# A seven-product attention/pooling step on one core: eight products in the first two chunks' attention stage, the combined weights made later, and stores moved to GpSimd's DMA queue

## The chip, the cores and the metric

The kernel runs on one core of a Trainium2 chip. The metric is the device time of one execution in microseconds (us). The time before is 2448.59 us, the median of 3 runs (2443.82 to 2450.43). A profiled execution of the same kernel took 2446.67 us.

Engines are named as the profile names them: PE is TensorE (matrix products), DVE is VectorE, ACT is ScalarE, POOL is GpSimd, and SP is SyncE, which in this kernel issues DMAs. Each engine runs its own instruction list strictly in order; an instruction that waits for a semaphore holds up everything behind it on its engine. In the lists, SPq and the like mean the instruction queue of that engine, where DMA issues stand.

## What is computed

One layer of a decoder step over 4096 prompt positions (and 8 single sampled positions), model width 1024, all in float32:

```python
u, zp, q, k, v, za, gp, ga = split_projection(rmsnorm(xp, g_norm[l]), w_in[l])
pooled = multiscale_pool(u, 0, seq)                        # trailing means, windows 2/4/8/16
att = attn_prompt(q, k, v, rel_bias, attn_sinks[l])        # 8 heads of 64, 2 kv heads, window 128, sinks
pg = jnp.einsum('btgc,gce->btge', pooled.reshape(b, t, POOL_GROUPS, POOL_GROUP_DIM), w_grp)
br_pool = jnp.einsum('btp,pd->btd', pg * pool_scale * jax.nn.silu(z_pool), w_br_pool)
br_attn = jnp.einsum('bta,ad->btd', att * jax.nn.silu(z_attn), w_br_attn)
merged = jax.nn.sigmoid(g_pool) * br_pool + jax.nn.sigmoid(g_attn) * br_attn
x + jnp.einsum('btd,de->bte', merged, w_out)               # then a final rmsnorm
```

The input projection `split_projection` is the largest matrix product: 1024 inputs, 4352 output columns. Its columns are cut into tiles of 128, named by their place in one array of weight tiles: `W_U`=0, `W_Z`=4, `W_Q`=8, `W_K`=12, `W_V`=13, `W_A`=14, `W_GP`=18, `W_GA`=34; `W_BR` and `W_O` belong to the two later products.

## The kernel before

**Numbers in two halves.** PE multiplies in a reduced format, so each operand is kept as a high part and a low rest, and every product is made of three matrix passes (`mm3`: high by high, high by low, low by high). The two halves of a weight tile are made by `split_into`: ACT copies the raw float32 tile into the high half (`w[:, 0]`), and DVE (or POOL, where it is told) subtracts to get the low half. The tile `w` (128 partitions, 4 KB each, 512 KB in all) comes from `wtile`: five buffers with the tag `w`, and from the second chunk on three more (`w2`), because `more_weights` closes a first memory pool (`p0`, whose tiles `fst` makes) at the end of the first chunk and opens another in its place.

**Seven products.** The sequence is cut into 8 chunks of 512 positions (the second has 520: the 8 sampled positions ride along). Within a chunk, two weight tiles (`ia`, `ib`) and the two halves of the chunk's columns form a 2 by 2 block product, done by class `Pair` with the Strassen-Winograd scheme: 7 block products rather than 8, each 12 matmuls of 256 columns (260 in the second chunk). `part1` makes four of them, `part2` three. Four of the seven weight operands are sums of quarter tiles: s1 to s4. In the first chunk `combined` loads the four quarters and DVE adds them (line 196); `kept` splits each sum and stores it to DRAM (`ss...`, line 169); from the second chunk on, `kept` loads the finished 512 KB tile with one DMA (line 165) and nothing is added. The other three operands are plain quarters, loaded as 256 KB and split each time (`wquarter`). DVE and ACT put the products of a pair together (lines 267 to 285).

**Order of a chunk.** (1) `K`: the key/value pair, two query pairs, the first attention-gate pair; meanwhile `finish` normalizes and stores the chunk before. (2) `S`, the attention stage: eight steps `hb`. Each does one pair out of `FILL` (`a`, `u`, `z`, `u`, `z`, `gp`, `ga`, `gp`): `part1`, then the earlier steps' value product and transposes, the scores of this step, then `part2`. These are the pairs that the change touches. From the second chunk on they make their low halves on POOL (`att`). Then the pair `ga 1`. (3) `B`: the two output branches for 8 tiles, with the last gate pairs between (`gate_pair`). (4) `O`: the output product, and the next chunk's input (`prep_xt`); in the first chunk its weights are split and stored too (`kept("o...")`).

**What sets the order.** The code names the work in one order, and a scheduler lists it for each engine in another: each instruction is put where its operands and buffers are expected to be free, with the code's order as priority. All DMAs stand in SP's list. Matmul results live in five PSUM buffers (`mm`): a pair in the first chunk takes two, in the second chunk (260 columns don't fit two to a buffer) four, and the scores take two per step.

## Time and profile before

| | before |
|---|---|
| median of 3 runs | 2448.59 us |
| the profiled execution | 2446.67 us |
| its span, first to last instruction | 2444.9 us |
| PE busy | 2363.1 us (97%) |
| DVE busy | 1650.8 us (68%) |
| ACT busy | 1146.0 us (47%) |
| POOL busy | 310.0 us (13%) |
| DMA | 583.60 MB, mean 239 GB/s |
| mean granted PE clock | 0.987 |

Busy time counts each engine by itself, so the four overlap. A busy share is a mean over stages with different limits; the prediction therefore reads windows, which give busy times between two moments of the span. The stages are cut where their first instruction of a kind starts: `K` at the first copy of line 614, `S` at the first score reduction (line 407), `B` at the first branch product (line 801), `O` at the first residual sum (line 847), up to the next chunk's line 614. `S` as cut here with what follows it up to `B` holds the eight steps, the pair `ga 1` and part of the next pair. For the first chunk these moments are 56.4, 96.7, 240.8 and 319.5 us, and the second chunk's are 375.6, 418.7, (end of its eight steps) 518.6, 546.5 and 625.6.

In a row of grouped instructions stand the line, the engine, the operation, output and inputs, the shapes, the count, the busy time, the mean duration in ns, and the idle time ahead of them with what ended it. In a row of waits stand who waited for whom, the total, the count and the longest. In a row of DMA issues stand the count, the size and the median time from issue to landing.

### The profile page before, as it was taken

The page shows a single profiled execution, that of the slowest core. Times are in us where ns is not written, and L with a number is a line of the kernel's source. Part 1 is how long each engine was busy: PE and PEld are TensorE (multiplying, and loading weights), DVE is VectorE, ACT ScalarE, POOL GpSimd, SP SyncE. Part 2 cuts the span into 40 slices and gives each one's busy share as a digit, 9 for nine tenths or more (in the row PEclk, how much of TensorE's full clock was granted, in tenths as well). Part 3 has the DMA queues.
Part 4 walks back from the last instruction along what each step waited for, and adds up shares of the span by engine and source line. Part 5 has one row for each costly group of instructions (what it writes and reads, how often), then busy time and mean ns, then how long its engine had stood idle before and what let it go on. Part 6 is the DMA issues. An engine that isn't in the chain of part 4 may idle for free.

```text
span 2444.9 us, 43970 instructions
## 1 busy us (share of the span) xinstructions
PE 2363.1 (97%) x16551; PEld 2198.0 (90%) x16551; DVE 1650.8 (68%) x3208; ACT 1146.0 (47%) x2324; POOL 310.0 (13%) x258
## 2 busy tenths in 40 slices
PE   7989999999999999999999999999999999999997
PEld 6878879999999988999889998899888998899986
DVE  6998776865668656686566855677556775668652
ACT  4667534563245633465234642456423563245531
POOL 0000001310024000330003300042001410013000
PEclk9989999999999999999999999999999999999998
DMA  6756688876686667767677666776667776687653
GB/s 203 255 194 245 226 282 322 227 244 219 223 279 239 237 231 242 272 232 245 212 256 266 236 229 233 246 267 237 228 233 260 248 239 231 233 279 246 215 196 141
DMA packets 231903, 583.60 MB, mean 239 GB/s; under 512 B 36315, under 2 KB 38652, under 8 KB 231692
## 3 DMA queue, kind: packets, MB, share of 16 engines
q1 hardware_dynamic: 231692, 580.80, 69.3%
q8 instruction: 131, 2.15, 0.3%
q14 instruction: 80, 0.66, 0.1%
HBM read 516.30 MB, written 64.40 MB: 238 GB/s over the span
## 4 chain that ended last, share of the span: by engine, by line
PE 68%; DVE 16%; DMA 7%; ACT 4%; issue 3%; SPq 0%; POOL 0%; DVEq 0%; ACTq 0%; POOLq 0%
PE hb L175 12%; PE hb L177 12%; PE hb L176 12%; PE mm L177 9%; PE mm L175 9%; PE mm L176 8%; DMA H<-in_xt 3%; DMA wr<-in_xq 2%; DVE oy L569 2%; DVE w L137 2%; PE tp L433 2%; PE pv L444 2%; DVE H L675 1%; DVE xt L180 1%; ACT LL L414 1%
## 5 line engine op out<-in xcount | busy, mean ns | idle before, releaser
L175 PE MATMUL hb<-xt,w 128*128 128x256 f32 x3316 | 945.3, 285 | 33.5 <-DVE U L268 13.3
L177 PE MATMUL hb<-xt,w 128*128 128x256 f32 x3316 | 941.4, 284 | 7.0 <-DVE w L137 7.0
L176 PE MATMUL hb<-xt,w 128*128 128x256 f32 x3316 | 938.2, 283 | 3.1 <-DVE xt L180 3.0
L175 PEld LDWEIGHTS hb<-xt,w 128*128 128x128 f32 x3316 | 633.2, 191 | 46.6 <-DVE H L272 15.1
L177 PEld LDWEIGHTS hb<-xt,w 128*128 128x128 f32 x3316 | 632.5, 191 | 10.1 <-DVE w L137 9.9
L176 PEld LDWEIGHTS hb<-xt,w 128*128 128x128 f32 x3316 | 632.8, 191 | 6.1 <-DVE xt L180 4.3
L136 ACT CAST w<-wr 128x512 fp32r<-128x512 f32 x570 | 349.5, 617 | 324.3 <-PE hb L177 202.2
L137 DVE TENSOR_TENSOR w<-wr,w 128x512 fp32r<-128x512 f32 x402 | 275.6, 689 | 141.1 <-ACT w L136 135.8
L137 POOL TENSOR_TENSOR w<-wr,w 128x512 fp32r<-128x512 f32 x168 | 251.6, 1501 | 500.5 <-ACT w L136 409.7
L175 PE MATMUL mm<-mh,w 128*128 128x512 f32 (+1 forms) x576 | 213.8, 371 | 2.4 <-ACT w L136 2.3
L177 PE MATMUL mm<-mh,w 128*128 128x512 f32 (+1 forms) x576 | 213.6, 371 | 0.8 <-DVE w L137 0.8
L176 PE MATMUL mm<-ml,w 128*128 128x512 f32 (+1 forms) x576 | 213.0, 370 | 0.3 <-DVE ml L809 0.3
L297 POOL TENSOR_TENSOR rs<-rs,nhalf 128x4 f32<-128x4 f32 (+1 forms) x18 | 17.9, 999 | 1338.9 <-DVE rs L295 1338.8
L801 DVE SCALAR_TENSOR_TENSOR H<-H,mm 128x512 f32<-128x512 f32 (+1 forms) x144 | 90.3, 628 | 111.9 <-PE mm L177 111.6
L414 ACT ACTIVATE LL<-LL,nm 128x257 f32<-128x257 f32 (+1 forms) x256 | 126.5, 496 | 65.9 <-DVE nm L411 65.8
L175 PE MATMUL mm<-xt,w 128*128 128x260 f32 x476 | 135.9, 286 | 2.0 <-DMA w<-ss 1.3
L177 PE MATMUL mm<-xt,w 128*128 128x260 f32 x476 | 134.8, 284 | 1.1 <-POOL w L137 0.6
L176 PE MATMUL mm<-xt,w 128*128 128x260 f32 x476 | 134.6, 283 | 0.0
L281 DVE TENSOR_TENSOR H<-hb,U 128x512 f32<-128x512 f32 x119 | 81.9, 688 | 73.3 <-PE hb L177 71.0
L175 PEld LDWEIGHTS mm<-mh,w 128*128 128x128 f32 x576 | 108.5, 188 | 22.4 <-ACT w L136 2.8
L177 PEld LDWEIGHTS mm<-mh,w 128*128 128x128 f32 x576 | 108.6, 189 | 22.0 <-DVE w L137 1.9
L847 DVE TENSOR_TENSOR oy<-mm,H 128x512 f32<-128x512 f32 (+1 forms) x72 | 45.1, 630 | 122.9 <-PE mm L177 93.1
(193 smaller groups left out, 4113.8 us busy)
## 6 DMA issues: line engine op xcount, KB each, us to landing
w<-ss SPq DMA_DIRECT2D x476, 512.0 KB, 4.4
wr<-in_wall SPq DMA_DIRECT2D x569, 256.0 KB, 3.4
w<-so SPq DMA_DIRECT2D x112, 512.0 KB, 4.0
ss<-w SPq DMA_DIRECT2D x68, 512.0 KB, 3.2
H<-in_xt SPq DMA_DIRECT2D x32, 512.0 KB, 5.6
wr<-in_xq SPq DMA_DIRECT2D x56, 256.0 KB, 3.0
H<-in_xt SPq DMA_DIRECT2D x56, 256.0 KB, 5.7
out_y<-oy SPq DMA_DIRECT2D x28, 512.0 KB, 4.6
```

What stands on the lines that cost most here:

```text
L136: nc.scalar.copy(w[:, 0], raw)
L137: (eng or nc.vector).tensor_tensor(out=w[:, 1], in0=raw, in1=w[:, 0].bitcast(F32), op=ALU.subtract)
L175: mm(ps, lhsT=w[:, 0, k0 + k, :], rhs=rh, start=start and k == 0, stop=False, **kw)
L176: mm(ps, lhsT=w[:, 0, k0 + k, :], rhs=rl, start=False, stop=False, **kw)
L177: mm(ps, lhsT=w[:, 1, k0 + k, :], rhs=rh, start=False, stop=stop and k == nk - 1, **kw)
L281: nc.vector.tensor_tensor(out=self.mid, in0=self.R, in1=u2.unsqueeze(1).to_broadcast([P, 2, n]), op=ALU.add)
L414: nc.scalar.activation(out=L[:, j, k0:2 * P + 1], in_=L[:, j, k0:2 * P + 1], func=AF.Exp, bias=nm[:, j:j + 1], accum_out=den[:, j:j + 1])
L433: nc.tensor.transpose(tp[:, j, :], L[:, j, kb * P:(kb + 1) * P], ident)
L444: mm(pv, lhsT=vs[:, b + kb, g, :], rhs=pt[:, kb, m].rearrange("p j q -> p (j q)"), start=n == 0 and m == 0, stop=n == len(kbs) - 1 and m == 1)
L569: nc.vector.scalar_tensor_tensor(out=y, in0=y, scalar=gf[:, e:e + 1], in1=rsp[:, 0:n], op0=ALU.mult, op1=ALU.mult)
L801: nc.vector.scalar_tensor_tensor(out=t[:, a:b], in0=t[:, a:b], scalar=1.0, in1=ps, op0=ALU.add, op1=ALU.mult)
L847: nc.vector.tensor_tensor(out=y[:, e % 4, a:f], in0=ps[:, 0:f - a], in1=xt[:, e % 2, a:f], op=ALU.add)
```

## The change

`PLAIN = 2`: in the first two chunks the eight pairs of `S` are made by eight plain block products (`eight1`, `eight2`) with the four raw quarters as operands, each quarter's split tile being used for two products one after the other. They use no sums, so nothing is combined, stored or loaded for them there. In the first chunk DVE makes the low halves, in the second POOL does, as for the other pairs of that stage. Each pair's results are put together by two ACT copies and two DVE additions.

The sums for these eight pairs, needed from the third chunk on, are made by `combine`: four raw loads, four additions, four splits, four stores for each. The code names it eight times in the second chunk: before each of its five gate pairs outside the eight steps, and in three places of its `O`. It uses buffers of its own from the first pool: four raw tiles (`wr0`), one sum (`sr`, made in place), one split tile (`sc`). Therefore `more_weights` now comes at the end of the second chunk, and the second chunk has five `w` buffers.

All stores of `kept` (85 in all: the sums, the pooling weight and the 16 output tiles) and the raw loads of `combine` (32) are issued by POOL; SP has none of them. In the first chunk's other pairs the sum buffer goes from two tiles to one, and s1 is made and used ahead of s2.

```diff
-    def kept(key, make):
-        w = wtile()
+    def kept(key, make, own=False):
+        w = fst([P, 2, 4, P], "sc", 1, F32R) if own else wtile()
...
-        nc.sync.dma_start(out=cache[key], in_=w.bitcast(F32))
+        nc.gpsimd.dma_start(out=cache[key], in_=w.bitcast(F32))
...
-    def combined(ia, ib):
-        odd = len(cache) // 4 % 2
+    def combined(ia, ib, own=False):
+        odd = own or len(cache) // 4 % 2
...
-            nc.sync.dma_start(out=raw[idx, half], in_=i["wall"][idx][:, 4 * half:4 * half + 4, :])
+            (nc.gpsimd if own else nc.sync).dma_start(out=raw[idx, half],
+                                                      in_=i["wall"][idx][:, 4 * half:4 * half + 4, :])
...
-        s1, s2 = [fst([P, 4, P], "sr", 2) for q in range(2)]
+        s = fst([P, 4, P], "sr", 1)
...
-        make = {"s2": lambda: add(s2, s1, a11, ALU.subtract), "s1": lambda: s1,
-                "s3": lambda: add(a21, a11, a21, ALU.subtract), "s4": lambda: add(s2, a12, s2, ALU.subtract)}
+        make = {"s1": lambda: add(s, a21, a22, ALU.add), "s2": lambda: add(s, s, a11, ALU.subtract),
+                "s3": lambda: add(a21, a11, a21, ALU.subtract), "s4": lambda: add(s, a12, s, ALU.subtract)}
...
+        def eight1(self):
+            for q, (p0_, p1_), e in (("11", (self.q6, self.q1), 1), ("21", (self.r5, self.r7), 3)):
+                w = self.w(q)
+                self.prod(p0_, q, B_11, True, w)
+                self.prod(p1_, q, T_1, not self.one, w)
+                nc.scalar.copy(self.q[e], p0_)
+
+        def eight2(self):
+            for q, (p0_, p1_), e in (("12", (self.q6, self.q1), 0), ("22", (self.r5, self.r7), 2)):
+                w = self.w(q)
+                self.prod(p0_, q, B_21, False, w)
+                self.prod(p1_, q, B_22, False, w)
+                nc.scalar.copy(self.q[e], p0_)
+                nc.vector.tensor_tensor(out=self.q[e + 1], in0=p1_, in1=self.q[e + 1], op=ALU.add)
+            return self.h
...
+    def combine(ia):
+        make, _ = combined(ia, ia + 1, True)
+        for q in ("s1", "s2", "s3", "s4"):
+            kept(f"{q}_{ia}", make[q], True)
...
+        later = [first_tile(*f) for f in FILL] if c == PLAIN - 1 else []
...
+            if later:
+                combine(later.pop(0))
             x = gate(which, p)
...
+            x = Pair(c, idx, idx + 1, off=16 if what == "u" else 0, eng=att, plain=c < PLAIN)
...
-        if c == 0:
-            more_weights()
...
+            if later and e in (1, 4, 7):
+                combine(later.pop(0))
+        if c == PLAIN - 1:
+            more_weights()
```

**How the lists move.** Line numbers from 31 on are a little higher in the changed kernel: 138 is the low half (before 137), 137 the high half (136), 170 the store (169), 192 the raw load (191), 198 the sums (196), 255, 262 and 263 the putting together in `eight1` and `eight2`.

First, DVE in the first chunk's attention stage, some twelve rows around the end of one pair. Before (the sums are rows with `sr`, the low halves rows of line 137):

```order
L196 TENSOR_TENSOR sr_1218<-wr_1210,wr_1212 128x512
L411 TENSOR_SCALAR nm_1135<-mx_1119 128x4
L196 TENSOR_TENSOR sr_1219<-sr_1218,wr_1214 128x512
L196 TENSOR_TENSOR wr_1210<-wr_1214,wr_1210 128x512
L417 RECIPROCAL rc_1142<-den_1137 128x4
L395 COPY LL_853<-skb 128x4
L281 TENSOR_TENSOR H_1038<-hb_1037,U_134_1039 128x2x256
L137 TENSOR_TENSOR w_1225<-sr_1219,w_1225 128x512
L675 TENSOR_TENSOR H_1199<-H_1038 128x2x527
L137 TENSOR_TENSOR w_1243<-wr_1214,w_1243 128x512
L675 TENSOR_TENSOR H_1200<-H_1199 128x525
L685 TENSOR_TENSOR H_1199<-H_1199,cf 128x16
```

and in the changed kernel:

```order
L448 TENSOR_SCALAR nm_1274<-mx_1258 128x4
L263 TENSOR_TENSOR H_1184<-hb_1182,H_1184 128x256
L138 TENSOR_TENSOR w_1485<-wr_1483,w_1485 128x512
L454 RECIPROCAL rc_1281<-den_1276 128x4
L432 COPY LL_849<-skb 128x4
L263 TENSOR_TENSOR H_1184<-hb_1183,H_1184 128x256
L658 SCALAR_TENSOR_TENSOR H_1349<-H_1349,H_1184 128x2x512
L138 TENSOR_TENSOR w_1516<-wr_1514,w_1516 128x512
L751 SCALAR_TENSOR_TENSOR H_1349<-mm_1359,psc,H_1349 128x512
L751 SCALAR_TENSOR_TENSOR H_1349<-mm_1364,psc,H_1349 128x512
L138 TENSOR_TENSOR w_1564<-wr_1562,w_1564 128x512
L138 TENSOR_TENSOR w_1594<-wr_1592,w_1594 128x512
```

The sums are gone from this stage, and a pair has four low halves where it had seven.

Second, POOL in the second chunk's attention stage. Before, with the low halves of that stage:

```order
L137 TENSOR_TENSOR w_4997<-wr_4995,w_4997 128x512
L137 TENSOR_TENSOR w_5074<-wr_5072,w_5074 128x512
L137 TENSOR_TENSOR w_5174<-wr_5172,w_5174 128x512
L137 TENSOR_TENSOR w_5206<-wr_5204,w_5206 128x512
L673 COPY H_5056<-carry 128x2x16
L627 CAST vs<-vs 128x256
```

and in the changed kernel, with the combining of weight tile 6 (`ss1_6` to `ss4_6` are its four sums in DRAM) among them:

```order
L138 TENSOR_TENSOR w_633_4897<-wr_632_4895,w_633_4897 128x512
L170 DMA ss3_6_6883<-sc_918_6879 128x1024
L732 COPY carry_89<-H_587_4548 128x32
L192 DMA wr0_990_7444<-in_wall 128x512
L138 TENSOR_TENSOR w_647_4971<-wr_646_4969,w_647_4971 128x512
L138 TENSOR_TENSOR w_649_5001<-wr_648_4999,w_649_5001 128x512
L170 DMA ss4_6_6889<-sc_919_6885 128x1024
L192 DMA wr0_1016_7683<-in_wall 128x512
L138 TENSOR_TENSOR w_660_5082<-wr_659_5080,w_660_5082 128x512
```

The code names the combining later, but the scheduler lists it far ahead, since its buffers are free: of the 32 splits into `sc`, 3 stand in the first chunk's `B`, 6 in its `O`, 6 in the second chunk's `K` and 17 among its eight attention steps. POOL's list there holds 32 low halves (before 24) and 17 stores, with the raw loads of the next combining between them.

Third, ACT in the same stage of the changed kernel, over two of the last steps (line 451 is the exponential, 262 and 255 the copies of a pair out of PSUM, 471 the transposed probabilities):

```order
L137 CAST sc_1047_7922<-sr_1046_7921 128x512
L262 COPY H_720_5549<-mm_716_5545 128x260
L137 CAST w_760_5873<-wr_759_5871 128x512
L451 ACTIVATE LL_556_4362,den_733_5650<-LL_556_4362,nm_732_5648 128x257 x4
L262 COPY H_720_5549<-mm_718_5547 128x260
L137 CAST sc_1048_7928<-sr_1046_7921 128x512
L457 ACTIVATE LL_556_4362<-LL_556_4362,rc_734_5655 128x256 x2
L780 ACTIVATE H_720_5549<-H_720_5549 128x2x520
L255 COPY H_743_5728<-mm_739_5724 128x260
L137 CAST w_778_5958<-wr_777_5956 128x512
L255 COPY H_743_5728<-mm_741_5726 128x260
L137 CAST sc_1049_7934<-wr0_1042_7913 128x512
```

Each row with `sc` writes the one `sc` buffer, so it waits until the store of the row with `sc` before it has landed; the PSUM copies and the exponentials stand behind it in ACT's list.

More of the change, by code (lines that the diff above doesn't have):

```diff
@@ L33 @@
 EPS = 1e-6
+PLAIN = 2
 NACT = 2
@@ L204, in split_kernel, with __init__ @@
     class Pair:
-        def __init__(self, c, ia, ib, off=0, eng=None):
-            self.c, self.ia, self.ib, self.eng = c, ia, ib, eng
+        def __init__(self, c, ia, ib, off=0, eng=None, plain=False):
+            self.c, self.ia, self.ib, self.eng, self.eight = c, ia, ib, eng, plain
             self.pre = {}
@@ L212, in __init__ @@
             self.one = 2 * n * 4 <= 2048
-            if c == 0:
+            if c == 0 and not plain:
                 self.make, self.plain = combined(ia, ib)
@@ L224, in __init__ @@
             self.mid = f[:, off + n:off + n + 2 * (SW - n)].rearrange("p (e t) -> p e t", e=2)[:, :, 0:n]
-            self.u2 = st([P, HB], "U2", 2)[:, 0:n]
+            if not plain:
+                self.u2 = st([P, HB], "U2", 2)[:, 0:n]
         def prefetch(self, *names):
@@ L235, in w @@
                 return kept(f"{q}_{self.ia}", self.make[q] if self.c == 0 else None)
-            if self.c == 0:
+            if self.c == 0 and not self.eight:
                 w = wtile()
@@ L274, in part2 @@
         def part2(self):
+            if self.eight:
+                return self.eight2()
             one, u2, n = self.one, self.u2, self.n
@@ L286, in part2, with first_tile @@
             return self.h
+    def first_tile(what, g):
+        if what in ("gp", "ga"):
+            return (W_GP if what == "gp" else W_GA) + 2 * g
+        return {"a": W_A, "u": W_U, "z": W_Z}[what] + g
+    def combine(ia):
+        make, _ = combined(ia, ia + 1, True)
+        for q in ("s1", "s2", "s3", "s4"):
+            kept(f"{q}_{ia}", make[q], True)
     def pair(c, ia, **kw):
@@ L736, in gate @@
         def gate(which, p, **kw):
-            idx = (W_GP if which == "gp" else W_GA) + 2 * p
+            idx = first_tile(which, p)
             return Pair(c, idx, idx + 1, **kw)
+        later = [first_tile(*f) for f in FILL] if c == PLAIN - 1 else []
         def gate_done(which, p, h):
@@ L777, in split_kernel @@
                 next(smp_steps)
+        if later:
+            combine(later.pop(0))
         x = gate("ga", 1)
@@ L871, in split_kernel @@
                 prep_xt(nxt, e // 2)
+            if later and e in (1, 4, 7):
+                combine(later.pop(0))
+        if c == PLAIN - 1:
+            more_weights()
         final = (c, acc, oy, n)
```

23 lines of the change are left out of this document (10 added, 13 removed).

## The prediction

> **What bounds the kernel now.** I read the page's first part, then windows by stage, then PE's waits.
>
> ```profile
> span 2444.9 us, 43970 instructions
> PE 2363.1 (97%) x16551; PEld 2198.0 (90%) x16551; DVE 1650.8 (68%) x3208; ACT 1146.0 (47%) x2324; POOL 310.0 (13%) x258
> ```
>
> PE is busy 97% of the span, so the kernel as a whole is bound by the number of matmuls, and an added matmul is an added time wherever PE doesn't wait. Windows by stage show where it does wait. The columns are the stretch, its length, each engine's busy time with its instructions, the granted PE clock, and the DMA share and rate. In order: the first chunk's `K`, `S` (to `B`), `B`, `O`; the second's `K`, eight steps, and the rest up to `O`; then `S` and `O` of the fourth chunk as a calm measure.
>
> ```profile
> core 0: us, PE busy (x) PEld busy (x) DVE busy (x) ACT busy (x) POOL busy (x), PEclk, DMA share, GB/s
> 56.40:96.70 40.30, 38.64 (x316) 37.28 (x315) 39.49 (x68) 23.49 (x41) 2.33 (x4) 1.00 0.79 283
> 96.70:240.80 144.10, 131.48 (x949) 121.08 (x948) 130.72 (x281) 99.84 (x227) 6.30 (x3) 0.94 0.61 220
> 240.80:319.50 78.70, 78.48 (x463) 68.77 (x462) 63.08 (x108) 39.34 (x73) 2.99 (x6) 1.00 0.61 215
> 319.50:375.60 56.10, 51.18 (x245) 41.37 (x245) 35.59 (x61) 19.05 (x30) 0.63 (x4) 0.97 0.93 335
> 375.60:418.70 43.10, 42.08 (x347) 41.35 (x346) 29.81 (x55) 20.66 (x43) 6.20 (x7) 1.00 0.90 321
> 418.70:518.60 99.90, 97.45 (x785) 94.74 (x784) 74.20 (x189) 57.08 (x138) 31.02 (x27) 1.00 0.77 233
> 518.60:625.60 107.00, 106.61 (x879) 105.81 (x878) 67.11 (x136) 46.82 (x90) 1.01 (x1) 1.00 0.66 225
> 1016.10:1137.80 121.70, 120.89 (x972) 117.72 (x971) 91.45 (x204) 76.42 (x177) 33.60 (x26) 1.00 0.71 244
> 1216.80:1266.80 50.00, 49.89 (x261) 42.26 (x260) 29.95 (x52) 14.63 (x21) 0.00 (x0) 1.00 0.73 247
> ```
>
> The first chunk's `S` takes 144.1 us against 121.7 in the fourth chunk. DVE is busy 130.7 of 144.1 there, PE idles 12.6, and the clock was granted at 0.94, which costs (1 - 0.94) x 144.1 = 8.6 us. Its `O` takes 56.1 against 50.0 with DMA at 0.93. In the second chunk's eight steps PE is busy 97.45 of 99.90: nothing is left to gain there. So the whole loss that this change could take away is some 25 us in the first chunk. What PE waits for in that `S`, and what holds SP's list in the first 376 us:
>
> ```profile
> PE hb L177 <- DVE w L137: 7.0, 6, 3.2
> PE hb L175 <- ACT w L136: 3.7, 7, 1.0
> ...
> SPq L169 <- DVE w L137: 131.7, 72, 11.7
> ```
>
> PE waits for weight halves. The stores in SP's list wait 131.7 us for them in total, with the next loads behind.
>
> **The change part by part.**
>
> *The eighth products* are certain. A product's first and twelfth matmul:
>
> ```profile
> 1040.61 0.28 PE L175 MATMUL hb<-xt,w 128*128 128x256 f32 x1
> ...
> 1041.91 0.28 PE L177 MATMUL hb<-xt,w 128*128 128x256 f32 x1
> ```
>
> Eleven steps take 1.30 us, so a product takes 1.42 us, and one of 260 columns 1.44 (x 260/256, an estimate). Eight pairs cost 11.3 us of PE in the first chunk and 11.5 in the second.
>
> *The first chunk's `S`.* Durations of DVE there, and of ACT's high half:
>
> ```profile
> L137 DVE TENSOR_TENSOR w<-wr,w 128x512 fp32r<-128x512 f32 x29 | 19.8, 687 | 1.1 <-ACT w L136 1.1
> L137 DVE TENSOR_TENSOR w<-sr,w 128x512 fp32r<-128x512 f32 x20 | 13.7, 687 | 3.8 <-ACT w L136 3.7
> L281 DVE TENSOR_TENSOR H<-hb,U 128x512 f32<-128x512 f32 x7 | 4.8, 687 | 2.9 <-PE hb L177 2.9
> L272 DVE TENSOR_TENSOR H<-hb,H 128x256 f32<-128x256 f32 x7 | 2.9, 418 | 0.0
> L268 DVE TENSOR_TENSOR U<-hb,U 128x256 f32<-128x256 f32 x7 | 2.9, 418 | 0.1
> ...
> L196 DVE TENSOR_TENSOR sr<-sr,wr 128x512 f32<-128x512 f32 x7 | 4.8, 689 | 0.1
> ...
> L136 ACT CAST w<-wr 128x512 fp32r<-128x512 f32 x98 | 59.5, 618 | 27.9 <-PE mm L177 11.3 <-DMA wr<-in_wall 8.1 <-PE hb L177 3.7
> ```
>
> A pair loses 4 sums and 3 low halves, 7 x 0.688 = 4.8 us of DVE. Putting it together took 3 x 0.42 + 0.69 = 1.95 us (line 271 as 272) and will take 2 x 0.42, another 1.1 us less. Eight pairs: 47 us. DVE's demand falls from 130.7 to about 84 us and it no longer bounds. At the fourth chunk's pace this stretch is worth 121.7 us, less about 2.7 for the 23 matmuls that the first block lacks (972 against 949, at 0.118 each); with the eighth products 119.0 + 11.3 = 130.3, so 13.8 us less than now. But the pairs `ga 1` and the one after it still combine, so some of the waits stay: I take -12, with -13.8 and -8 as the ends.
>
> *The single sum buffer* puts an ACT copy (0.62 us) between s1 and s2, and the next pair's s1 behind s4. In the first chunk's `K` DVE is busy 39.49 of 40.30 us, so this is on the path: 4 pairs x 2 x 0.62 = 5 us if nothing stands between, less than nothing (PE's 1.7 us idle) if the freed SP list helps more. I take +1. In `B` DVE has 15 us to spare, which hide it and the 3 early splits and their sums (7 x 0.69 = 4.8 us, the price if the cover were gone). Moving the stores gains by itself at most those idle times, since SP's queue is seen by PE only through late halves.
>
> *More transfers where DMA is fullest.* Into the first chunk's `O` go about 4 stores of 0.52 MB and 4 raw loads of 0.26, 3.1 MB; into the second chunk's `K` about 6 and 8, 5.2 MB.
>
> ```profile
> ss<-w SPq DMA_DIRECT2D x37, 512.0 KB, 3.7
> ...
> w<-ss SPq DMA_DIRECT2D x8, 512.0 KB, 7.1
> ...
> GB/s 357 308 316 65 0 171 388 251 346 335 418 388 378 336 146 249 285 163 399 335 224 392 418 426 394 397 340 329 363 399 395 335 257 281 266 319 407 418 426 418
> w<-ss SPq DMA_DIRECT2D x15, 512.0 KB, 5.5
> ```
>
> `O` moves 335 GB/s x 56.1 = 18.8 MB now and will move 21.9; `K` 321 x 43.1 = 13.8, then 19.0. At the best rate of a slice above, 426 GB/s, that is 51 and 45 us, 1.5 more than `K` has. At 335/0.93 = 360 GB/s it is 61 and 53, 14 us more than both have. Below nothing: `O` loses up to its 4.9 us of idle PE if loads no longer stand behind stores. I take +4, nearer to the slices, since stores may land late, but loads then land late too: 5.5 us in that `K`, 7.1 for those issued in `O`.
>
> *Five `w` buffers in the second chunk* give a load the time of 4 products, 5.8 us. A landing of 5.5 fits; one of 7.1 is 1.3 late, for 16 such loads 21 us. After `S` the DMA share was 0.66, so there it is hidden. I take +1, since 5.5 is that stage's own median.
>
> *The second chunk's eight steps*: +11.5. POOL makes 32 low halves there instead of 24 and issues 17 stores and about as many loads among them. Its durations (min/median/max) in the third chunk's steps, and a DVE operation of the same stretch:
>
> ```profile
> L137 POOL TENSOR_TENSOR w<-wr,w x24: 1285/1318/2232, 705.1 to 806.3; 128x512 fp32r<-128x512 f32 x24
> ...
>   ACT w L136: 57.9, 18
> ...
> L423 DVE TENSOR_SCALAR LL<-LL,rc x14: 336/350/1394, 727.2 to 806.4; 128x256 f32<-128x256 f32 x14
> ```
>
> 32 halves are 42 us at the median and 71 if each were the longest. What a DMA issue costs POOL isn't in this trace: from nothing to 1.3 us, a half's price; 35 of them give up to 46 us, and the 111 us of the stage hold 42 and 46. DVE loses 8 x 1.26 us of pair sums (5 x 0.42 against 2) and gets 4.25 combinings, 17 x 2 x 0.69 = 23 us: 74 becomes 88 of 111. Neither is a bound by its sum.
>
> The *chain through the one `sc` buffer* may be. Each link is an ACT copy 0.62, a DVE low half 0.69, a wait behind a POOL half of 0.65 on average, the issue of 0 to 1.3, and the landing, 3.7 in the first chunk's `S`: 5.7 to 7.0 us. The lists place 17 links among the eight steps, 111.4/17 = 6.55 us for each. ACT's copy into `sc` waits for the landing, and the copies that free a pair's PSUM buffers, and the exponentials, stand behind it; PE waits for those. From nothing to 17 x 0.4 = 7 us; I take +4, about the middle.
>
> The rule of the Trainium skill that speaks against this stands in "SBUF — State Buffer", section "SBUF: two separate sides": descriptors of a DMA from GpSimd's queue are written by software through a port pair that VectorE's fast modes lock, and such DMAs should go to SP or ACT. The trace bears out the lock for computing: line 423 takes 0.35 us alone and up to 1.39, in a stretch where POOL's halves take up to 2.23; no run here shows it for descriptors. By it each store could be up to 1 us later, 17 us in the chain.
>
> The sum: +1 - 12 + 0 + 4 + 1 + 11.5 + 4 = +9.5 us, from 2446.67 to 2456.2 us for the profiled execution. The median of the runs stands 1.9 us above that execution, so I predict 2448.6 + 9.5 = 2458 us; 0.3%, about what a measurement of this kernel can tell from no change, is 7.3 us.
>
> **The rivals.**
>
> *All is hidden.* Transfers and chain find room: -13.8 + 11.5 = -2.3 us, 2446 us, not slower. For it: DMA slices of 426 GB/s, ACT busy only 57 of 99.9 us in the second chunk's steps. Against it: 441 GB/s are asked in `K`.
>
> *The chain binds.* A link that also waits once behind another ACT and another DVE instruction of 0.6 takes 8.4 us; (8.4 - 6.55) x 17 = 31 in place of 4 gives +36.5 us, 2485 us. It decides from a link of 6.55 us on. For it: POOL's low halves ahead of a store wait themselves for ACT (57.9 us in 18 waits above). Against it: a pair's PSUM copy has some 2.9 us of slack, two products, before PE needs the buffer.
>
> By the Trainium skill, "DMA: Bandwidth & Descriptors", section "SWDGE vs HWDGE vs iDMA", the descriptors are computed on GpSimd's cores; this would lengthen each link. No run here shows by how much.
>
> *Transfers bind* at 360 GB/s: 14 for the two stages and 5 for late loads, in place of 4 and 1, and nothing for the chain, which waits less where PE is slower: 9.5 + 14 - 4 = +19.5 us, 2468 us. For it: the 0.93 in `O`. Against it: the slices.
>
> *The first chunk gives back everything*: its `S` 13.8, its `O` the 6.1 us above the fourth chunk's, its `K` 1.7, the second chunk pays 11.5: -10 us, 2438.5 us. For it: the 131.7 us of stores ahead of loads in SP's list. Against it: `O` gets more bytes, not fewer.
>
> **How the numbers follow.** The forecast has a chance of 0.35 (its own range 2450 to 2466), "all is hidden" 0.25, "the chain binds" 0.17, "transfers bind" 0.12, "everything back" 0.11. Slower by over 0.3% (above 2455.9): two thirds of the forecast, the chain and the transfers, 0.53. Faster (below 2441.2): 0.11, the last case. Within: 0.36. The range 2440 to 2481 leaves out the upper part of the chain's case and the lower part of the last, about 0.2 together.
>
> **What would show it.** In the first chunk's `S`: near 132 us, DVE busy under 90, no granted clock under 0.97. The second chunk's eight steps: near 115 us; if ACT's waits for stores of `sc` lead PE's waits there, the chain binds. First `O` and second `K`: 56 to 62 and 43 to 46 us; more means transfers. From the third chunk on nothing should move by over 2 us. The forecast is wrong in sign if the first chunk's `S` falls below 125 us, or if its `O` falls to 50.

## The result, and the profile after

The changed kernel takes 2490.53 us (median of 4 runs, 2486.44 to 2491.14), and the kernel before, beside it, 2446.97 us (4 runs, 2443.82 to 2450.43): a ratio of 1.0174, 95% interval 1.0155 to 1.0193. It is slower by 43.6 us, where the prediction said 9.5; 2490.5 lies above the range (2440 to 2481). The page's first lines of the kernel after, whose profiled execution is the source of all rows of "after" below:

```profile
span 2489.4 us, 44409 instructions
PE 2381.9 (96%) x16743; PEld 2221.8 (89%) x16743; DVE 1659.2 (67%) x3176; ACT 1164.0 (47%) x2372; POOL 383.7 (15%) x383
```

PE's busy time rose by 18.8 us (2381.9 against 2363.1), the span by 44.5. So more than half of the loss is PE waiting. The windows by stage, cut as those of before: the first chunk's `K`, `S` (to `B`), `B`, `O`; the second's `K`, eight steps, and the rest up to `O`.

```profile
57.70:99.90 42.20, 38.37 (x306) 36.53 (x305) 37.23 (x61) 24.11 (x43) 7.21 (x15) 1.00 0.68 244
99.90:231.50 131.60, 130.00 (x1047) 126.53 (x1047) 96.21 (x216) 89.24 (x215) 7.93 (x12) 1.00 0.35 123
231.50:322.70 91.20, 81.74 (x462) 70.34 (x462) 68.65 (x117) 42.32 (x80) 18.22 (x34) 0.96 0.67 236
322.70:387.00 64.30, 53.05 (x247) 44.30 (x247) 42.59 (x73) 22.74 (x37) 13.87 (x30) 0.87 0.93 342
387.00:439.90 52.90, 43.19 (x331) 41.43 (x330) 35.05 (x56) 22.94 (x48) 12.98 (x17) 0.97 0.85 309
439.90:566.10 126.20, 115.40 (x889) 111.75 (x888) 98.13 (x204) 74.13 (x176) 57.40 (x63) 0.96 0.54 172
566.10:675.40 109.30, 108.22 (x893) 107.41 (x892) 70.13 (x140) 49.74 (x95) 1.57 (x2) 1.00 0.68 230
```

Against the rows of before: the first `S` is 12.5 us shorter, and then `B` is 12.5 longer, `O` 8.2, the second `K` 9.8, and the eight steps 26.3. From the third chunk on only the `K`s and one `O` (the fifth chunk's, 54.2 before and 50.2 after) move by over 2 us; they differ by up to 4 us either way with the clock granted in them (a late `K` takes 39.7 to 39.8 us at 1.00 and 43.2 to 43.5 at 0.92), in the runs below too. So one stage of one profile is read to some 3 or 4 us, no closer.

### The profile page after: what moved, and what is told of

It is laid out like the page before. It is cut to its first block, busy times and chain, and to the rows that moved or that the text cites. A ratio compares the mean times of both kernels' runs of the same rounds, so it can differ in the third digit from the quotient of the medians.

```text
span 2489.4 us, 44409 instructions
## 1 busy us (share of the span) xinstructions
PE 2381.9 (96%) x16743; PEld 2221.8 (89%) x16743; DVE 1659.2 (67%) x3176; ACT 1164.0 (47%) x2372; POOL 383.7 (15%) x383
## 3 DMA queue, kind: packets, MB, share of 16 engines
q1 hardware_dynamic: 215996, 521.54, 61.6%
## 4 chain that ended last, share of the span: by engine, by line
PE 61%; DVE 9%; DMA 5%; ACT 2%; issue 2%; POOL 0%; SPq 0%; DVEq 0%; ACTq 0%; POOLq 0%
PE hb L176 11%; PE hb L177 11%; PE hb L178 11%; PE mm L176 7%; PE mm L178 7%; PE mm L177 7%; DMA H<-in_xt 2%; DVE oy L606 2%; DMA wr<-in_xq 2%; PE pv L481 2%; PE tp L470 1%; DVE H L712 1%; PE S L439 1%; PE S L440 1%; DVE w L138 1%
## 5 line engine op out<-in xcount | busy, mean ns | idle before, releaser
L138 DVE TENSOR_TENSOR w<-wr,w 128x512 fp32r<-128x512 f32 x402 | 275.5, 687 | 145.3 <-ACT w L137 141.2
L138 POOL TENSOR_TENSOR w<-wr,w 128x512 fp32r<-128x512 f32 x176 | 261.8, 1491 | 468.8 <-ACT w L137 370.1
L334 POOL TENSOR_TENSOR rs<-rs,nhalf 128x4 f32<-128x4 f32 (+1 forms) x18 | 18.7, 1038 | 1228.3 <-DVE rs L332 1228.3
L176 PE MATMUL mm<-xt,w 128*128 128x260 f32 x508 | 149.1, 294 | 19.9 <-DMA w<-ss 14.5
L178 PE MATMUL mm<-xt,w 128*128 128x260 f32 x508 | 147.3, 290 | 1.0 <-POOL w L138 1.0
L177 PE MATMUL mm<-xt,w 128*128 128x260 f32 x508 | 147.0, 289 | 0.0
L177 PEld LDWEIGHTS mm<-ml,w 128*128 128x128 f32 x576 | 108.8, 189 | 21.9 <-DVE ml L847 1.9
```

Of the source, the lines that this page charges most:

```text
L138: (eng or nc.vector).tensor_tensor(out=w[:, 1], in0=raw, in1=w[:, 0].bitcast(F32), op=ALU.subtract)
L176: mm(ps, lhsT=w[:, 0, k0 + k, :], rhs=rh, start=start and k == 0, stop=False, **kw)
L177: mm(ps, lhsT=w[:, 0, k0 + k, :], rhs=rl, start=False, stop=False, **kw)
L178: mm(ps, lhsT=w[:, 1, k0 + k, :], rhs=rh, start=False, stop=stop and k == nk - 1, **kw)
```

## The experiments

Fourteen kernels were run. The table gives the stages of each in us (second chunk: `K`, eight steps, then `Y+B+O`, all that follows up to the third chunk; `Y` is the stretch between the eight steps and `B`). Where the time is a median, the 95% interval of its ratio to the kernel before stands beside it; the others had one run and a profile.

| kernel | time | ratio | K | S | B | O | K 2nd | eight steps | Y+B+O 2nd |
|---|---|---|---|---|---|---|---|---|---|
| before | 2447 | | 40.2 | 144.2 | 78.7 | 56.1 | 43.1 | 99.9 | 161.8 |
| after | 2490.5 | 1.0155–1.0193 | 42.1 | 131.6 | 91.2 | 64.3 | 52.9 | 126.3 | 162.4 |
| 1 stores only on GpSimd | 2466.1 | 1.0068–1.0099 | 41.8 | 149.5 | 82.7 | 59.6 | 45.4 | 102.0 | 162.3 |
| 2 no combining | 2463.8 | 1.0047–1.0101 | 42.1 | 132.3 | 85.6 | 60.1 | 44.3 | 112.9 | 163.9 |
| 3 combining without stores | 2472.2 | | 42.9 | 130.9 | 86.5 | 63.4 | 49.9 | 115.4 | 164.1 |
| 4 combining's DMAs on SP | 2477.3 | | 42.2 | 132.4 | 88.0 | 61.6 | 42.6 | 123.8 | 163.8 |
| 5 all DMAs on SP | 2467.7 | 1.0065–1.0102 | 42.1 | 130.7 | 81.1 | 56.7 | 44.7 | 125.9 | 165.6 |
| 6 no combining, all on SP | 2451.0 | 1.0003–1.0031 | 42.1 | 130.3 | 81.5 | 56.3 | 44.4 | 112.8 | 164.4 |
| 7 stores on ACT's queue | 2484.6 | | 43.9 | 164.0 | 84.0 | 57.8 | 43.4 | 105.2 | 162.7 |
| 8 low halves on POOL | 2453.6 | 1.0005–1.0027 | 41.6 | 148.1 | 80.1 | 56.7 | 43.3 | 99.9 | 161.6 |
| 9 two store buffers | 2482.9 | | 42.1 | 133.2 | 79.7 | 61.6 | 46.1 | 124.0 | 167.6 |
| 10 four pairs, one buffer | 2491.2 | 1.0156–1.0202 | 42.7 | 158.0 | 97.1 | 61.2 | 45.6 | 99.9 | 165.1 |
| 11 three pairs, one buffer | 2480.6 | 1.0105–1.0150 | 42.6 | 167.4 | 88.6 | 56.0 | 44.1 | 100.3 | 162.3 |
| 12 four pairs, shared buffers | 2467.7 | 1.0051–1.0101 | 42.7 | 145.3 | 91.1 | 61.3 | 43.8 | 99.9 | 161.2 |
| 13 combining in shared buffers | 2501.2 | | 42.1 | 130.1 | 80.6 | 56.5 | 45.3 | 112.9 | 212.8 |
| 14 only `O`'s stores on GpSimd | 2456.7 | | 40.2 | 143.7 | 81.8 | 60.4 | 44.4 | 102.1 | 162.1 |

### First round: is it the chain, the queue or the transfers?

Number 1 is the kernel before with one line changed:

```diff
-        nc.sync.dma_start(out=cache[key], in_=w.bitcast(F32))
+        nc.gpsimd.dma_start(out=cache[key], in_=w.bitcast(F32))
```

> The kernel before with one line changed: kept's 85 stores are issued by POOL instead of SP; seven products everywhere, nothing combined later. Theory chain (the loss comes from the combining's 32 splits, one after the other through one sc buffer): no loss here, 2440 to 2450 us, a few us better if SP's loads no longer stand behind stores. Theory queue (a store on POOL's queue is late by itself, and the first chunk waits for it in its w buffers): slower, 2455 us or more, the loss in the first chunk's K, B and O. Theory traffic (bytes where DMA is fullest): the same bytes as before, no change.

It is 19 us slower, by that line alone. The chain theory had said that nothing would come of it, and the prediction too had given this move no loss. Number 2 leaves out the combining (later chunks load another pair's tiles in its place); 3 keeps it without its 32 stores, with the same loads; 4 puts its raw loads and stores on SP:

```diff
-            kept(f"{q}_{ia}", make[q], True)
+            cache[f"{q}_{ia}"] = cache[f"{q}_{W_K}"]        # number 2, and no `combined`
...
+        if own:
+            cache[key] = cache[f"{key[:2]}_{W_K}"]          # number 3, ahead of the store
+            return w
...
+        (nc.sync if own else nc.gpsimd).dma_start(out=cache[key], in_=w.bitcast(F32))   # number 4
```

> The changed kernel without the combining: the 32 combined tiles of the attention stage are never made or stored, and the later chunks load the stored tiles of another pair in their place (same sizes), so the values of those pairs are not the reference's. What is left: eight products in two chunks, stores on POOL, one sum buffer, five w buffers in the second chunk. Chain and traffic: first chunk's attention stage -12.6 us as measured, second chunk's +11.5, little else: 2443 to 2452 us. Theory queue or five w buffers: the loss stays where the ordinary stores or loads are, 2465 us or more, seen in the first chunk's B and the second chunk's K and B.

> The changed kernel with the combining's loads, sums and splits, but its 32 stores left out; the later chunks load another pair's stored tiles, so those pairs' values are not the reference's. Chain: a link loses its landing of some 4.4 us, the lists run through; second chunk's eight steps near 113 us (126 now), first chunk's B near 80 (91), total 2448 to 2460 us. Traffic: two thirds of the added bytes gone, first O and second K give back some two thirds of 18 us, but the second chunk's eight steps, at a DMA share of 0.54, stay above 122: total 2470 to 2480 us. Engine load (sums and splits on DVE and ACT themselves): 2480 us or more.

> The changed kernel with the combining's loads and stores (64 DMAs) issued by SP instead of POOL; the other stores stay on POOL. Chain: a link loses POOL's part (a low half ahead of it, 0.65 us on average, and the issue of 0.56) and some of the landing, but SP's list then holds loads behind stores that wait: 2470 to 2490 us, the eight steps above 118. Queue: the loss is POOL's, so it falls to 2460 us or less.

Number 2 still loses 17 us, where the chain theory wanted 2443 to 2452; at 2463.8 it is just under the queue theory's 2465, and its loss stands in `B` and `O`. Number 3's eight steps fell to 115.4 us, near what the chain theory said, but its time stayed 25 us above before, and its `B` at 86.5 (said: near 80). It doesn't isolate the chain either: without landings to wait for, the scheduler lists the combining earlier. Splits into `sc` that are left in number 3's eight steps, in a list of the tile's instructions (after had 16 there):

```profile
L137 ACT CAST sc<-sr x5: 619/620/623, 430.8 to 455.3; 128x512 fp32r<-128x512 f32 x5
L137 ACT CAST sc<-wr x2: 622/626/629, 433.6 to 448.2; 128x512 fp32r<-128x512 f32 x2
```

Number 4 came out where the chain theory had it (2470 to 2490, eight steps above 118): 2477.3, with the eight steps at 123.8 us. With POOL's queue out of the chain the steps hardly move, so POOL's issue isn't what lengthens them. The second `K`, though, fell from 52.9 to 42.6.

### Second round: the queue taken out of the change

Number 5 is the kernel after with every store and raw load back on SP, number 6 the same without the combining, number 7 the kernel before with its stores on ACT's queue, which like SP's is served by hardware:

```diff
-        nc.gpsimd.dma_start(out=cache[key], in_=w.bitcast(F32))
+        nc.sync.dma_start(out=cache[key], in_=w.bitcast(F32))       # 5 and 6; in 7 nc.scalar
```

> The kernel after, with every store and every raw load back on SP's queue; the eight products, the one buffer for stores of combined pairs and the combining stay. Queue theory (the stores lose 17 to 19 us because on a queue of their own they overlap with the loads that SP goes on to issue, and both land later): the run with the combining's 64 transfers on SP stood at 2477, and the remaining stores' move is worth 17 to 19 of that, so 2456 to 2464, with the first chunk's B back near 80 us and the second chunk's K near 44. Chain theory (what is lost is the one-buffer chain, on whatever queue): 2470 or more, eight steps of the second chunk at 120 us or more and the other stages as in the kernel after. A third way: SP's queue now holds reloads behind stores that wait for the one buffer, and the two effects trade places: 2475 to 2490, with the loss in the second chunk's K and in its eight steps.

> The kernel after without the combining in the second chunk (raw loads, sums, splits and stores of the sixteen attention pairs are left out, and later chunks load another pair's tiles in their place) and with the stores on SP: what is left of the change is eight products for seven in two chunks, the single sum buffer and the order of the head's prefetch. Queue theory: the first chunk's S is 11 to 12 us shorter, the second chunk's eight steps 11 to 13 longer, nothing else moves: 2440 to 2452. Chain theory says the same. Give-back theory (the first chunk's B or O loses what S gains, since its combining and transfers run against the same limit however S ends): 2455 to 2462, with B or O of the first chunk 8 us or more longer.

> The kernel before with its stores issued by ACT and not by SP, nothing else changed. If the loss of the run with the stores alone on GpSimd (19 us) comes from any second queue, because loads no longer wait in line behind stores: 2455 to 2470, B and the second K 3 us or more longer, landing of stores near 4.4 us as there. If it comes from GpSimd (its own issue time, its software queue): within 6 us of before, 2441 to 2453, landing near 3.2 us. ACT also has its own work behind each store that waits for a half; that would show as ACT's waits at the store's line in the eight steps of the later stages.

Windows of number 5, the first chunk's `B`, `O`, the second's `K` and eight steps, and then the eight steps of number 6:

```profile
229.90:311.00 81.10, 79.48 (x464) 68.71 (x464) 68.22 (x117) 42.80 (x79) 4.66 (x5) 1.00 0.75 261
311.00:367.70 56.70, 50.54 (x246) 41.73 (x245) 37.34 (x64) 19.30 (x31) 0.90 (x6) 0.97 0.90 318
367.70:412.40 44.70, 42.07 (x331) 41.07 (x330) 31.07 (x49) 21.61 (x44) 7.91 (x7) 0.96 0.87 295
412.40:538.30 125.90, 115.64 (x893) 111.08 (x892) 95.20 (x201) 73.74 (x175) 43.22 (x35) 0.97 0.59 177
```

```profile
411.50:524.30 112.80, 110.66 (x886) 107.09 (x885) 67.02 (x171) 66.10 (x159) 41.21 (x35) 1.00 0.35 92
```

Number 5 ended between its theories' ranges (to 2464 for the queue, from 2470 for the chain). With everything on SP, `B`, `O` and the second `K` are back within 0.6 to 2.4 us of before; the eight steps keep all of their loss. But its scheduler also listed the combining elsewhere. Splits into `sc` that start in each stage, counted in the traces, and the data moved:

| kernel | `B` | `O` | `K` 2nd | eight steps | later | MB in `B` | MB in `O` | MB in `K` 2nd |
|---|---|---|---|---|---|---|---|---|
| before | 0 | 0 | 0 | 0 | 0 | 17.0 | 18.8 | 13.8 |
| after | 4 | 6 | 5 | 16 | 1 | 21.5 | 22.0 | 16.4 |
| 3 | 6 | 10 | 9 | 7 | 0 | 19.5 | 20.3 | 15.3 |
| 4 | 4 | 4 | 1 | 16 | 7 | 21.4 | 20.0 | 13.2 |
| 5 | 5 | 0 | 1 | 15 | 11 | 21.2 | 18.0 | 13.2 |

So `B` and the eight steps hold nearly the same combining in after and in 5, `O` and the second `K` don't.

Number 6 shows that eight products for seven in two chunks nearly cancel (`S` down 14, eight steps up 12.9, +3.6 in all). After, 5, 2 and 6 are the four cases with and without the combining, with the queue moved or not. From number 6 on: the queue alone adds 12.8 us (2 less 6), the combining alone 16.7 (5 less 6), both together 39.5 (after less 6), 10 more than their sum, which is about the noise of the four medians. The stages show it more sharply: `B`, `O` and the second `K` together take 182.2 us in number 6, 190.0 with the queue alone, 182.5 with the combining alone, and 208.4 with both. Of the 43.6 us, then, some 4 are number 6's, 17 the combining's on SP (13 of them in the eight steps), and 23 come with the queue: 13 of these by itself, the others only with the combining, partly because the scheduler then puts more of it into `O` and the second `K`.

What delays PE in the eight steps is ACT's copies out of PSUM (line 262), which free the buffers that the scores (`S`) need. PE's largest wait there in after and in number 6:

```profile
PE S L439 <- ACT H L262: 6.9, 3, 4.6
```

```profile
PE S L438 <- ACT H L262: 1.6, 1, 1.6
```

Nor is all of the loss waiting. In number 5's eight steps PE is busy 115.6 us for 893 matmuls at a granted clock of 0.97, in number 6's 110.7 for 886 at 1.00; in the first `O` of after 53.1 us for 247 at 0.87, in number 5's 50.5 for 246 at 0.97. Whether PE's waits bring the clock down was not tested.

Number 7 says that late landings aren't GpSimd's software alone. Its time, 2484.6 us, is above the ranges of both theories: `S` grew by 20 us, probably because ACT now waits for halves ahead of each store, so it is no clean price of a second queue. Its `B` also grows by 5.3 us, and its stores land late. Landings in the first chunk's `O` of before, of number 7, and of after, in rows of DMA issues:

```profile
so<-w SPq DMA_DIRECT2D x11, 512.0 KB, 3.0
H<-in_xt SPq DMA_DIRECT2D x6, 256.0 KB, 6.0
```

```profile
so<-w ACTq DMA_DIRECT2D x10, 512.0 KB, 6.4
H<-in_xt SPq DMA_DIRECT2D x6, 256.0 KB, 9.0
```

```profile
so<-w POOLq DMA_DIRECT2D x11, 512.0 KB, 7.5
ss<-sc POOLq DMA_DIRECT2D x6, 512.0 KB, 6.5
wr<-in_wall POOLq DMA_DIRECT2D x7, 256.0 KB, 8.8
```

On a second queue of either kind a store lands after 6.4 to 7.5 us where 3.0 sufficed, and the loads of the next chunk's input on SP land after 9.0 us for 6.0 (the raw weight loads in that `O` didn't change: 5.2 before, 5.1 in number 7). And the loads gained little by it. SP's waits for low halves at its raw loads up to the end of `O`, before and number 1:

```profile
SPq L149 <- DVE w L137: 14.6, 11, 2.8
SPq L191 <- DVE w L137: 10.5, 14, 2.7
```

```profile
SPq L191 <- DVE w L137: 89.6, 34, 9.8
SPq L149 <- DVE w L137: 63.4, 30, 9.5
```

The stores' 131.7 us in SP's list are gone, but the raw loads' waits for the same low halves rose from 25 to 153 us, since a raw tile is free only when its half is made. The stores had mostly held back loads that the buffers hold back anyway.

### A side trial: relief for DVE from POOL

If `S` is bound by DVE, some low halves could simply go to POOL, as in later chunks (number 8):

```diff
-                split_into(w, self.plain[q])
+                split_into(w, self.plain[q], self.eng)
...
-        att = nc.gpsimd if c else None
+        att = nc.gpsimd
```

> The kernel before, with the first chunk's attention pairs left at seven products, but the low halves of the splits of their plain quarters, the sums of their activations and the other operations that the later chunks give to GpSimd given to it in the first chunk too. The first chunk's eight attention steps are bound by VectorE; some 24 low halves of 0.69 us go, 16 us, and TensorE's 110.5 us go toward 99, the length in the second chunk. Queue theory (B lost in the kernel after because of the stores' queue, not because S ended sooner): 2434 to 2441. Give-back theory: the stage behind loses what this one gains: 2444 to 2450. Third: GpSimd becomes late itself, since its split of a half is slower than VectorE's: 2447 to 2455, with the low halves named in the waits of the stage.

`S` grew by 3.9 us. Windows of the first part of `S`, before and number 8, and then grouped instructions of number 8 there:

```profile
96.60:207.10 110.50, 98.87 (x711) 91.37 (x710) 100.50 (x223) 74.22 (x174) 6.30 (x3) 0.92 0.57 207
```

```profile
97.20:208.10 110.90, 94.55 (x707) 88.44 (x708) 99.40 (x203) 73.33 (x174) 34.13 (x24) 0.97 0.58 206
```

```profile
L137 POOL TENSOR_TENSOR w<-wr,w 128x512 fp32r<-128x512 f32 x21 | 33.4, 1602 | 72.4 <-ACT w L136 61.8 <-DVE sza L454 7.4 <-DMA ss<-w 1.9
...
L137 DVE TENSOR_TENSOR w<-sr,w 128x512 fp32r<-128x512 f32 x20 | 17.3, 867 | 6.1 <-ACT w L136 6.0
...
L196 DVE TENSOR_TENSOR sr<-sr,wr 128x512 f32<-128x512 f32 x6 | 5.1, 846 | 0.1
```

Twenty-one halves left DVE, 21 x 0.687 = 14.4 us, but DVE was busy only 1.1 us less (99.4 against 100.5): the mean of its own halves of sums rose from 687 to 867 ns and that of some of its sums from 689 to 846, while POOL's halves took 1602. The trace shows when: ten of the twenty DVE halves `w<-sr` ran beside a half on POOL and took 1049 ns in the mean, the other ten 685. Operations with an input in PSUM (`H<-hb,U`, 687) didn't change. So what POOL took over, DVE gave back in longer operations, and the third theory's range (2447 to 2455) held.

### Third round: the chain against the combining's own work

Number 9 is number 5 with two `sc` buffers, for which one `w` buffer is given up. Numbers 10 and 11 take eight products for only some of the first chunk's pairs, combine those in the first chunk, and leave the second at seven products:

```diff
-        w = fst([P, 2, 4, P], "sc", 1, F32R) if own else wtile()
+        w = fst([P, 2, 4, P], "sc", 2, F32R) if own else wtile()       # 9, with 4 `w` buffers for 5
...
-PLAIN = 2
+PLAIN = 1
+EIGHT = (1, 3, 5, 7)                                                   # 10; in 11 (2, 4, 6)
...
-            x = Pair(c, idx, idx + 1, off=16 if what == "u" else 0, eng=att, plain=c < PLAIN)
+            x = Pair(c, idx, idx + 1, off=16 if what == "u" else 0, eng=att, plain=c < PLAIN and hb in EIGHT)
```

> The run with every store on SP (2467.7, eight steps of the second chunk 125.9), with two buffers for the stores of combined pairs in place of one, and four `w` buffers in place of five, since memory holds no more. Chain theory (each split waits until the store before it has landed): the eight steps fall toward the 115.4 of the run without these stores, 113 to 118, the wait of ACT's high half for the store's landing (16.4 us in eight waits) falls under 5, total 2455 to 2462. Traffic or plain work theory (the 13 us over the run without combining are ACT's, VectorE's and the transfers' own time): 122 or more, 2463 to 2472. If the four `w` buffers bind, the loss shows in other stages of both chunks, above all where the weight loads are waited for.

> Eight products for four of the first chunk's eight attention pairs, every second one; the other four stay at seven. The four are combined in the first chunk itself, through the one buffer, and the second chunk has seven products throughout; every store is on SP, and the second memory pool opens after the first chunk as in the kernel before. The first chunk's S loses 4 x 3.6 us of VectorE (28.6 us went for eight pairs) and gains 4 x 1.4 of TensorE, so 94 to 99 us where before had 110.5. Thirteen of the sixteen splits with their sums, 13 x 1.4 = 18 us of VectorE, stand in Y and B, where VectorE idles 3 + 16 us. Hidden theory: total 2436 to 2443. Give-back theory: Y and B grow by what S loses, 2445 to 2452.

> As the run with four of eight pairs at eight products, with three (the third, fifth and seventh). VectorE loses 10.8 us of 100.5 in the first chunk's S, so 96 to 101 us; twelve splits with their sums, 16.5 us of VectorE, stand behind its scores, ten of them in Y. Hidden theory: 2436 to 2443. Give-back theory: Y is bound by VectorE (30.3 of 33.7 us) and grows by 8 or more, 2443 to 2450.

ACT's wait for landings in the eight steps, after, number 5 and number 9:

```profile
ACT sc L137 <- DMA ss<-sc: 16.5, 8, 4.2
```

```profile
ACT sc L137 <- DMA ss<-sc: 16.4, 8, 4.4
```

```profile
ACT sc L137 <- DMA ss<-sc: 5.6, 3, 4.0
```

The second buffer removed 10.8 us of waits, and the steps became 1.9 us shorter. They hold 19 splits there in place of 15, and PE's wait for ACT's copies (line 262) went from 3.3 us in number 5 to 8.3. The `w` buffer given up shows later: the third chunk's attention steps took 99.8 us for 91.7 and the fourth's 97.7 for 92.9, so the time, 2482.9, lies above both ranges. The run favours the work theory in the eight steps without measuring its share.

Numbers 10 and 11 failed both their theories by more than 25 us, and number 10 shows the chain where nothing hides it. Its first eight steps fell from 110.5 us to 91.1, but the stretch from there to `B` grew from 33.7 to 66.9. Eight splits stand in that stretch, but only three of them in a row that waits for landings (the expectation of number 12 speaks of eight). ACT in order of time there (start, duration, what, idle time before), and what PE waited for in that stretch:

```profile
229.61 0.62 ACT L138 CAST sc<-sr 128x512 fp32r<-128x512 f32 x1 [2.42 <-DMA ss<-sc]
233.90 0.62 ACT L138 CAST sc<-wr 128x512 fp32r<-128x512 f32 x1 [3.67 <-DMA ss<-sc]
238.20 0.62 ACT L138 CAST sc<-sr 128x512 fp32r<-128x512 f32 x1 [3.69 <-DMA ss<-sc]
```

```profile
PE hb L177 <- ACT w L138: 21.2, 2, 15.7
```

A link takes 4.3 us on SP's queue. The next product's high half stands behind the links in ACT's list, and PE waits 15.7 us in one piece for it. The two waits are 21.2 of the 33 us; PE's 288 matmuls also ran at a granted clock of 0.77.

Numbers 12 and 13 are 10 and 5 with the splits of combined pairs in the shared `w` buffers, so that there is no chain; the combining then stands where the code names it. Number 14 is the kernel before with only the `o...` stores on GpSimd:

```diff
-        w = fst([P, 2, 4, P], "sc", 1, F32R) if own else wtile()
+        w = wtile()                                                    # 12 and 13
...
-        nc.sync.dma_start(out=cache[key], in_=w.bitcast(F32))
+        (nc.gpsimd if key[0] == "o" else nc.sync).dma_start(out=cache[key], in_=w.bitcast(F32))   # 14
```

> The run with four of eight pairs at eight products (2491: S 91.1, but Y 66.9 for 33.7, where eight splits stand in a row in ACT's list and each waits for the landing of the store before it, 4.3 us a link), with the splits of combined pairs in the shared `w` buffers and not in one buffer of their own. Chain theory (Y's 35 us are eight links of 4.3): S stays near 91, Y returns to 31 to 40, Y, B and O together stay under 185 (before 168.5), total 2436 to 2452. Work theory (the additions, splits and transfers of four pairs cost as much behind S as in it): Y, B and O together 188 or more, 2455 or more.

> The run with every store on SP (2467.7), with the splits of combined pairs in the shared `w` buffers: the combining then stands where the code names it, in the second chunk's Y, B and O, and not in its eight attention steps. If the eight steps lost 13 us to the combining, by its chain or its work there, they come to 112 to 114, the first chunk's B and O and the second K to the lengths of the run without combining (81.5, 56.3, 44.4). Chain theory: Y, B and O of the second chunk grow by 10 us or less together, 2455 to 2465. Work theory: they grow by 13 to 30, since 32 splits and 32 additions, 44 us of VectorE, stand in stages that use 63 of 79 and 36 of 55 us of it: 2465 to 2485.

> The kernel before, with the sixteen stores of the first chunk's O on GpSimd's queue and all others left on SP. Queue theory (each stage loses where its stores no longer stand in line with its loads): B, Y and the attention stages as before, O longer by 3 to 4 us and the second K by 1 to 3, landing of these stores near 7 us where 3.0 was, total 2449 to 2455. If the loss of the run with all stores moved (19 us) lies in O's late buffers alone: 2458 or more. If it needs the stores of S: within 2 us of before.

Number 12's `S`, `B` and `O` sum to 297.7 us, number 10's to 316.3 and before's to 279.0. So without the chain 18.6 of 37.3 us went away, and 18.7 us of net loss remain with four combinings moved behind the scores (the stretch up to `B` is still 54.2 us where the chain theory had 31 to 40). The combining then shares its `w` buffers with the loads, so this remainder isn't the additions' and splits' alone. Number 13's eight steps are at 112.9, as without combining, and what follows them grew by 48 us against number 6. Its windows of the second chunk's `B` and `O`, and PE's waits in both:

```profile
560.40:662.80 102.40, 85.70 (x659) 84.48 (x659) 63.22 (x123) 36.54 (x68) 1.41 (x1) 0.93 0.79 272
662.80:737.70 74.90, 58.89 (x446) 58.16 (x446) 43.05 (x87) 20.71 (x32) 0.00 (x0) 0.90 0.80 287
```

```profile
PE mm L176 <- DMA w<-ss: 13.6, 3, 5.5
PE mm L176 <- DMA w<-so: 9.5, 3, 6.6
PE hb L176 <- DMA w<-ss: 6.5, 1, 6.5
```

DVE was busy 63 of 102 and 43 of 75 us: there was room beside PE, and PE waited 29.6 us for weights, whose loads stand in SP's list among the combining's stores and share its `w` buffers. PE's own work also took 12 us more than in number 6 for about as many matmuls (144.6 us for 1105 at clocks of 0.93 and 0.90, against 132.2 for 1103 at 1.00). Both theories had missed this; the work theory's cause (DVE) was wrong too.

Number 14 loses 9.0 us, half of number 1's 19, with `S` as before: `B` +3.1 (where the first of these stores stand), `O` +4.3, the rest just behind. The queue theory had `B` as before and 2455 us at most. So the loss follows the stores from stage to stage. Waits in its `O`:

```profile
DVE H L369 <- DMA H<-in_xt: 9.5, 4, 6.8
...
PE mm L175 <- ACT xt L384: 8.0, 1, 8.0
```

In `O` the loss is one chain: the next chunk's input (its loads land after 9.0 us, as in number 7, where before had 6.0) comes late to DVE and ACT, and PE waits 8.0 us in one piece.

No run beat the kernel before. Eight products save the first chunk some 14 us in `S` and cost the second 12.9, and in every place that was tried the combining came to 16.7 us or more; where half of the pairs changed and the second chunk paid nothing, moving four combinings out of `S` cost more than `S` gained.

## Why the prediction was wrong

The sign was right, and two terms held. The rest was low by 34 us, above all because the moved queue was given no cost. The steps:

- **First `S`, -12: right.** 131.6 us, said "near 132", at a clock of 1.00. DVE fell to 96, not to 84. Durations had been added up to the 47 us, and DVE's records overlap: in this window they sum to 151.4 us before and 108.0 after, 43 less, where busy time, which counts an overlap once, fell by 34.5. The other 4 us are six sums of these pairs that had stood ahead of the window. It made no difference, as PE was now busy 130.0 of 131.6.
- **Eighth products, second chunk, +11.5: right**; 12.9 in number 6. With the single sum buffer and the five `w` buffers (+1 each) the terms gave number 6 +1.5; it measured +3.6, or 0.7 to 7.6 by its interval.
- **"Moving the stores gains by itself at most those idle times, since SP's queue is seen by PE only through late halves": the largest error.** The sentence bounds a gain and has no term for a loss. The move costs 19 us in the kernel before (number 1), 12.8 in the changed kernel without the combining and 22.9 with it. The 131.7 us in SP's list were read as loads held back; most of these loads had no free raw tile to land in.
- **`B`, 0 ("hides it"): wrong by 12.5.** The cover was DVE's idle time, and for DVE it held: number 5 has the same combining in `B` at +2.4. What wasn't covered was the queue, which costs 10 us there.
- **`O` with the second `K`, +4: low by 14.** They lost 18. The queue alone costs 5.2 of it (number 2); the rest appears only where the combining stands in these stages on POOL's queue (after, and number 3 without the stores). Number 5 can't tell which part of the combining does it, since it holds one split there where after has eleven. So the rival "transfers bind" (14 us for the two) stays open: `O` moved the 22 MB that were said, at 342 GB/s, near the 360 of that rival; against it, `K` moved 16.4 MB for the 19.0 that were said, at only 309.
- **Eight steps, chain +4: low by 9.** The combining costs 13 us there (125.9 against 112.8). The chain's waits are there as described, 16.5 us in eight pieces, and PE waits for the copies that stand behind them, 6.9 us for 1.6 without the combining; but the part of ACT's waits that two buffers took away changed little. What the prediction probably left out is that the instructions put into ACT's and DVE's lists delay the copies behind them even where neither engine is full: "Neither is a bound by its sum" was true and not enough. How the 13 us divide between chain and work wasn't settled: number 9 changed the `w` buffers as well, and number 3 moved the work.
- **The rival "the chain binds", 2485, came nearest in time, for a wrong reason.** It put 31 us of chain into the eight steps, where the combining cost 13; another 23 us came with the queue, where it saw nothing. POOL's issue, bounded by 1.3 us, takes 0.53 to 0.59, and the steps are as long with POOL in the chain as with SP (126.3, 125.9). Issues of after in the eight steps (shortest, median, longest in ns):

```profile
L170 POOL DMA_DIRECT2D ss<-sc x16: 531/565/591, 445.3 to 564.5; - x16
```

- **The Trainium skill's rule** ("SBUF — State Buffer", section "SBUF: two separate sides") advised against the queue that lost, and its advice was sound here. But it lost mainly outside the chain, where the prediction applied the rule, and number 7 lost in `B` and in landing times on a queue that isn't software's.

## What to carry to other kernels

A queue full of stores that wait isn't lost time until a trace shows that the loads behind them had free buffers; here they hadn't, and the second queue only made stores and some loads land later. Idle engines didn't hide inserted work whose instructions stood in the lists of the engines that PE's next operand came through: look at what stands behind the inserted wait in that list, and at the buffer and the queue that the inserted stores share. Price a moved queue with one run that moves nothing else, and count in each run's trace where the inserted work stands before comparing stages: a scheduler that lists by free buffers moves it whenever a queue or a buffer changes.

## What the runs showed of the hardware that wasn't expected

A 512 KB store landed after 3.0 us (median) in `O` when issued from the loads' own queue, 6.4 from ACT's and 7.5 from POOL's: the step from the own queue to another was larger here than that between the two kinds. And POOL's low halves slowed those of DVE's operations with two inputs in SBUF that ran beside them (1049 ns for 685 in ten of twenty halves) and took 1.60 us themselves, so that 21 of them relieved DVE by 1.1 us; the Trainium skill, "SBUF — State Buffer", section "SBUF: two separate sides", says that the two engines share a port pair under an exclusive lock, also for VectorE operations with two inputs in SBUF against a GpSimd operation that reads it, which these rows bear out.
